# The block products of neighbouring column pairs in another order, raw weights in ten rotating homes, and a first pair computed K tile by K tile

## The chip, the core and the metric

The kernel runs on one core of a Trainium2 chip. Engines run beside each other: TensorE (PE, matmuls), VectorE (DVE) and ScalarE (ACT) for elementwise work, GpSimd (POOL) for some DMA issues, SyncE (SP) for most DMA issues. Each engine works through its own instructions in order, and semaphores tie the engines together. The metric is the device time of one execution in microseconds; the kernel before took 2662.76, 2666.23 and 2669.75 us in three runs (median 2666.23).

## What is computed

A trunk of two layers, each a half-step FFN, a token mixer (convolution, spatial gating, attention) and a second half-step FFN, for 576 tokens of width 1024. The change is in the FFNs; `D_FF` is 2816.

```python
def rms_norm(x, g):
    y = xf * lax.rsqrt(jnp.mean(xf * xf, axis=-1, keepdims=True) + EPS)
    return y.astype(x.dtype) * g
def swiglu(x, w_gu, w_down):
    gu = x @ w_gu
    return (jax.nn.silu(gu[..., :D_FF]) * gu[..., D_FF:]) @ w_down
def decoder_layer(...):
    x = x + 0.5 * swiglu(rms_norm(x, n1), gu1, dn1)
    m, ... = token_mixer(rms_norm(x, nm), ...)
    x = x + m
    x = x + 0.5 * swiglu(rms_norm(x, n2), gu2, dn2)
```

## The kernel before

Activations lie transposed, features on 128 partitions and the 576 tokens along the free axis, in two half columns of 288. A product in float32 quality takes three matmuls, since weights and activations are split into a high and a low part (`xh`, `xl`): high by high, high by low, low by high. K runs over 8 tiles of 128 for width 1024.

**Plain and block products.** The gate column and the up column of one index j (0 to 21) make a pair. Done plainly (`ftile`, lines 321 to 333, matmuls at L303, L306, L309), a pair takes 2 x 8 x 6 = 96 matmuls of 128x288. Only the first `N_PLAIN` = 2 pairs of the first FFN are done so. Every other pair is done as seven block products of 12 matmuls each (84), a scheme in the manner of Strassen: `product`, matmuls at L536, on sums of weight blocks and of activation blocks (`fac["b"]`, built by `post_x2`, `bottom`, `first_factors`). A pair needs a PSUM tile `z` with the two banks `z[:,0]` and `z[:,1]`, and a third bank `c`, called `n`. The seven products are called p1 to p7 here, by the bank that they add into:

- p1 into c (weights item q = 0), then ACT copies c into `z[:,0]`
- p5 into `z[:,1]` (q = 1), then ACT copies `z[:,1]` out into the buffer `p5`
- p6 into c (q = 3), then DVE writes `z[:,1]` = c + p5
- p2 into `z[:,0]` (q = 2)
- p7 into c (q = 4), then DVE writes u = c + p5
- p3 into `z[:,1]` (q = 5), then DVE writes g = z times the reciprocal norm `rstd`
- p4 into c (q = 6), then DVE takes u = c times `rstd` and finishes the pair (tanh on ACT, two products, a split into `ah` and `al`)

Each copy or sum between two products is a hand-over: the next product that writes one of its banks waits for it. `begin`, `middle` and `end` write the products of a pair; the scheduler orders instructions by priority, and the steady order on PE is p6(j), p1(j+1), p2(j), p5(j+1), p7(j), p3(j), p4(j).

**Weights.** A list `items` holds all weight pieces in order of use; `advance` loads each raw piece (256 KB) by a DMA on SP 4 items ahead of its preparation, and prepares it 7 items ahead of its use in the FFNs. To prepare is to split it: ACT writes the high part, DVE the low part (`by_vector`), or a DMA on POOL adds the raw piece onto minus the high part (`by_dma`, for q = 0, 2 and 6). The weights of the other four products are sums of raw blocks, made by DVE first (`sums`). Raw pieces live in `wr` (4 buffers), `cb` (4, shared with the mixer's convolution and its `ml`) and `vT` (1, shared with the attention); for pairs, the parity of j chooses `wr` or `cb`. The prepared forms rotate over the tags `w`, `sp`, `w`, `pt`.

**The FFN's start and end.** The 22 pairs are worked in four chunks; behind each chunk its products with the down projection (`w_dn`) follow. At the very start, x arrives tile by tile; ACT splits each tile and squares it (`post_x`), and the squares are summed on DVE. `rstd_steps` turns the sum into `rstd`: PE sums over partitions (`m<-ones,sq`), DVE does Newton steps on a 128x5 tile, PE spreads the result (`m<-idr,oh`), ACT copies it out. Behind the mixer the eight tiles of x come one by one out of the products with `w_out`, and `post_x2` builds the blocks from each.

Of the kernel before, what the change touches and what calls it, by code (L numbers as in the profile page):

```python
# [16 lines left out]
P = 128  # L17
# [23 lines left out]
W_G, W_C = (4, 4, 2, 3), (2, 3, 2)  # L41
CHUNKS = ((0, 6), (6, 12), (12, 17), (17, KF))

N_PLAIN = 2
# [51 lines left out]
def trunk(ctx: ExitStack, tc: tile.TileContext, a):  # L96
# [67 lines left out]
    def plain(ap, n, ff=False):  # L164
        for k0 in range(0, n, 4):
            items.append(("plain_ff" if ff else "plain", ap[:, k0:min(k0 + 4, n), :], min(n - k0, 4)))
# [4 lines left out]
    def ffn_items(l, f):  # L171
        j0 = N_PLAIN if l == 0 and f == 0 else 0
        for j in range(2 * j0):
            plain(a["w_gu"][l, f, j], 8, True)
        for k0, k1 in chunks(l, f):
            last = None
            for j in range(max(k0, j0), k1):
                for i, q in ((j, 0), (j, 1), (last, 4), (last, 5), (last, 6), (j, 3), (j, 2)):
                    if i is not None:
                        items.append(("pair", (l, f, i), q))  # L180
                last = j
            for q in (4, 5, 6):
                items.append(("pair", (l, f, last), q))
            for m in range(KD):
                plain(a["w_dn"][l, f, m, :, k0:k1, :], k1 - k0, True)

    for l in range(L):
# [12 lines left out]
        for i in range(8):  # L200
            plain(a["w_out"][l, i], 8)
        ffn_items(l, 1)
    state = {"load": 0, "prep": 0, "use": 0}
    state["form"] = 0
    raws, ready = {}, {}

    def load_raw(i):
        kind, what, n = items[i]

        def raw(key, ap, n, home="wr"):  # L210
            if home == "wr":
                t = wp.tile([P, 4, P], F32, tag="wr", name="wr", bufs=4)[:, 0:n, :]
            elif home == "cb":
                t = sp.tile([P, CB], F32, tag="cb", name="wc", bufs=4)[:, 0:n * P].rearrange("p (k m) -> p k m", k=n)
            else:
                t = sp.tile([P, 5, P], F32, tag="vT", name="wv")[:, 0:n, :]
# [5 lines left out]
        else:  # L222
            l, f, j = what
            for h, k in {0: ((0, 0),), 1: ((1, 0), (1, 4)), 2: ((0, 4),)}.get(n, ()):
                home = ("wr", "cb")[j % 2] if (h, k) != (1, 4) else ("wr", "cb", "vT")[j % 3]
                raw((what, h, k), a["w_gu"][l, f, 2 * j + h, :, k:k + 4, :], 4, home)

    def parts(ff, n):
        tag = "w"
        if ff:  # L230
            tag = ("w", "sp", "w", "pt")[state["form"] % 4]
            state["form"] += 1
# [20 lines left out]
    def prepare(i):  # L253
        kind, what, n = items[i]
        if kind != "pair":
            ready[i] = by_vector(raws.pop(i), n, kind == "plain_ff")
            return
        a11, a12, a21, a22 = (raws.get((what, h, k)) for h, k in ((0, 0), (0, 4), (1, 0), (1, 4)))
# [23 lines left out]
    def advance(i, look, raw=4):  # L282
# [38 lines left out]
    def ftile(rh, rl, z=None):  # L321
        z = z or ztile()
        zc = z if isinstance(z, list) else [z[:, c, 0:HT] for c in range(2)]
        k, nk = 0, len(rh)
        while k < nk:
# [4 lines left out]
            for g in list(chains):  # L330
                if next(g, "end") == "end":
                    chains.remove(g)
# [150 lines left out]
    for k in range(KD):  # L483
        sy.dma_start(out=x[k], in_=a["x"][:, k, :])
        if k in (0, 3):
            advance(0, 0 if k == 0 else 2, 0)
        post_x(k, 0, V_N1)
# [52 lines left out]
    def ffn(l, f, nxt):  # L540
        start = l == 0 and f == 0
        p5 = sp.tile([P, 2, 384], F32, tag="ws", name="p5")
        r = None
        for k0, k1 in chunks(l, f):
# [19 lines left out]
            def begin(what):  # L564

                b, j = fac["b"], what[2]
                z, c = ztile(), mtile("n")[:, h1]
                o = {"z": z, "c": c, "what": what, "p5": p5[:, j % 2, h1]}
                product(c, weights(what, 0), b[0], True)
                se.activation(out=z[:, 0, h1], in_=c, func=AF.Copy)  # L570
                product(z[:, 1, h1], weights(what, 1), b[1], True)
                se.activation(out=o["p5"], in_=z[:, 1, h1], func=AF.Copy)
                return o

            def middle(o):

                b, z, c, what = fac["b"], o["z"], o["c"], o["what"]
                product(c, weights(what, 3), b[3], False)
                ve.tensor_tensor(out=z[:, 1, h1], in0=c, in1=o["p5"], op=ALU.add)
                product(z[:, 0, h1], weights(what, 2), b[2], False)  # L580

            def end(o):

                b, z, c, what = fac["b"], o["z"], o["c"], o["what"]
                product(c, weights(what, 4), b[4], False)
                u = slot("t", "u")
                ve.tensor_tensor(out=u[:, h2], in0=c, in1=o["p5"], op=ALU.add)
                product(z[:, 1, h1], weights(what, 5), b[5], False)
                g, t = gate(z)
                product(c, weights(what, 6), b[6], False)  # L590
                silu(g, t)
                ve.tensor_tensor(out=u[:, h2], in0=u[:, h2], in1=r[:, h2], op=ALU.mult)
                ve.tensor_tensor(out=u[:, h1], in0=c, in1=r[:, h1], op=ALU.mult)
                keep(u, t)

            last = None
            for j in range(k0, k1):
                if start and j < N_PLAIN:
                    z = [ftile(xh, xl), ftile(xh, xl)]
                    if j == 0:  # L600
                        r = rms()
                        tops = first_factors()
                    g, t = gate(z[0])
                    silu(g, t)
                    u = slot("t", "u")
                    ve.tensor_tensor(out=half(u), in0=zf(z[1]), in1=half(r), op=ALU.mult)
                    keep(u, t)
                    if j == N_PLAIN - 1:
# [571 lines left out]
```

## Time and profile before

| what | value |
|---|---|
| three runs, median | 2666.23 us (2662.76 to 2669.75) |
| profiled execution: its own time, its span | 2666.37 us, 2664.6 us |
| busy: PE, DVE, ACT, POOL | 98%, 71%, 48%, 11% of the span |
| mean granted TensorE clock | 0.986 |
| chain of work that ended last | PE 82%, DVE 7%, DMA 7%, issue 3%, ACT 1% |

A matmul's row in the trace gives its start and its duration; matmuls overlap, so what one costs is read from starts or from a stretch with a count. The releaser in brackets behind a row is what ended the idle time ahead of it. A granted clock of 1.00 is 2.4 GHz, 0.50 is 1.2 GHz. PE is at 9 tenths or more in all of the page's 40 slices but the first.

### The profile page before, as it was taken

Reading aid. Unit: us, or ns where it says so; the run is one execution under the profiler, and the core shown is the slowest. Engines: PE = TensorE matmul, PEld = TensorE weight load, DVE = VectorE, ACT = ScalarE, POOL = GpSimd, SP = SyncE. Lnnn points to the kernel's source line nnn. Section 1 sums busy time; section 2 is a strip of 40 time slices with the busy share of each in tenths; the row PEclk is TensorE's granted clock in tenths of the full one; section 3 lists DMA queues with packets and bytes.
Section 4 is the critical chain, followed back from the end, with each engine's and each line's share of the span. In section 5 each row is a group of like instructions: output and inputs, shape, how many; then the busy total and the mean of one; then the engine's idle time right before and its main releaser. Section 6 shows DMA issues by size and latency. Waiting matters only on the chain.

```text
span 2664.6 us, 49246 instructions
## 1 busy us (share of the span) xinstructions
PE 2608.1 (98%) x18984; PEld 2533.2 (95%) x18984; DVE 1902.2 (71%) x3494; ACT 1283.6 (48%) x2423; POOL 291.6 (11%) x320
## 2 busy tenths in 40 slices
PE   6999999999999999999999999999999999999999
PEld 6999999988899989999989999999888999999999
DVE  6675665588898776756786766746888977756765
ACT  5454453335524464644674644533454245644543
POOL 0111110020010010111110111100200100111110
PEclk7999999989999999999999999999899999999999
DMA  5464554231222464654554645632312234645643
GB/s 166 113 152 120 131 123 135 81 92 57 60 82 82 122 143 120 151 124 119 134 129 117 151 119 124 135 126 84 82 56 68 84 91 128 151 119 133 138 122 100
DMA packets 194352, 304.08 MB, mean 114 GB/s; under 512 B 39482, under 2 KB 56762, under 8 KB 194116
## 3 DMA queue, kind: packets, MB, share of 16 engines
q1 hardware_dynamic: 156820, 233.28, 28.8%
q0 software_dynamic: 37152, 67.65, 15.2%
q8 instruction: 149, 2.44, 0.4%
q14 instruction: 87, 0.71, 0.1%
q10 hardware_dynamic: 144, 0.00, 0.0%
HBM read 221.43 MB, written 8.84 MB: 86 GB/s over the span
## 4 chain that ended last, share of the span: by engine, by line
PE 82%; DVE 7%; DMA 7%; issue 3%; ACT 1%; POOL 0%; SPq 0%; DVEq 0%; POOLq 0%; ACTq 0%
PE z L303 17%; PE z L306 17%; PE z L309 17%; PE n L536 13%; PE z L536 12%; PE n L86 4%; PE m L86 2%; DVE u L88 2%; DVE w L88 2%; DMA w<-wr 1%; DMA w<-wc 1%; DMA wv<-w_gu 1%; DMA w<-wv 1%; DMA wc<-w_gu 1%; DVE sums L88 1%
## 5 line engine op out<-in xcount | busy, mean ns | idle before, releaser
L88 ACT ACTIVATE w<-wr 128x512 fp32r<-128x512 f32 x762 | 433.5, 584 | 813.3 <-PE z L309 630.7
L536 PE MATMUL z<-xh,w 128*128 128x288 f32 x2064 | 455.8, 300 | 9.7 <-DVE z L88 6.5
L88 DVE TENSOR_TENSOR w<-wr,w 128x512 fp32r<-128x512 f32 (+2 forms) x528 | 321.3, 609 | 160.4 <-ACT w L88 159.5
L536 PEld LDWEIGHTS z<-xh,w 128*128 128x128 f32 x2064 | 343.6, 189 | 24.6 <-DVE z L88 13.4
L303 PE MATMUL z<-xh,w 128*128 128x288 f32 x1504 | 336.3, 305 | 13.5 <-ACT w L88 9.7
L88 DVE TENSOR_TENSOR w<-sums,w 128x512 fp32r<-128x512 f32 x344 | 235.4, 688 | 148.4 <-ACT w L88 145.9
L309 PE MATMUL z<-xh,w 128*128 128x288 f32 x1504 | 326.8, 298 | 0.1
L306 PE MATMUL z<-xl,w 128*128 128x288 f32 x1504 | 326.7, 299 | 0.0
L536 PE MATMUL z<-xl,w 128*128 128x288 f32 x1032 | 305.2, 296 | 0.0
L536 PE MATMUL n<-fh,w 128*128 128x288 f32 x1376 | 304.7, 295 | 0.1
L303 PE MATMUL z<-ah,w 128*128 128x288 f32 x1408 | 303.0, 297 | 0.0
L306 PE MATMUL z<-al,w 128*128 128x288 f32 x1408 | 301.8, 296 | 0.0
L309 PE MATMUL z<-ah,w 128*128 128x288 f32 x1408 | 301.1, 296 | 0.0
L303 PEld LDWEIGHTS z<-xh,w 128*128 128x128 f32 x1504 | 245.6, 193 | 26.8 <-issue 10.1
L88 ACT ACTIVATE w<-sums 128x512 fp32r<-128x512 f32 x344 | 212.9, 623 | 121.0 <-PE z L309 76.0
L306 PEld LDWEIGHTS z<-xl,w 128*128 128x128 f32 x1504 | 247.1, 192 | 0.9 <-issue 0.7
L309 PEld LDWEIGHTS z<-xh,w 128*128 128x128 f32 x1504 | 246.2, 192 | 0.8 <-issue 0.3
L88 DVE SCALAR_TENSOR_TENSOR c<-cb,vec,c 128x512 f32<-128x512 f32 x480 | 243.5, 553 | 0.1
L536 PEld LDWEIGHTS n<-fh,w 128*128 128x128 f32 x1376 | 230.8, 188 | 0.6 <-DVE w L88 0.3
L303 PEld LDWEIGHTS z<-ah,w 128*128 128x128 f32 x1408 | 226.4, 189 | 3.2 <-ACT ah L88 3.2
L309 PEld LDWEIGHTS z<-ah,w 128*128 128x128 f32 x1408 | 226.5, 189 | 0.0
L306 PEld LDWEIGHTS z<-al,w 128*128 128x128 f32 x1408 | 226.4, 189 | 0.0
(244 smaller groups left out, 4598.2 us busy)
## 6 DMA issues: line engine op xcount, KB each, us to landing
wr<-w_in SPq DMA_DIRECT2D x184, 256.0 KB, 2.8
wr<-w_gu SPq DMA_DIRECT2D x168, 256.0 KB, 3.0
wc<-w_gu SPq DMA_DIRECT2D x156, 256.0 KB, 3.0
wr<-w_dn SPq DMA_DIRECT2D x128, 256.0 KB, 2.7
w<-wr POOLq DMA_DIRECT2D x117, 256.0 KB, 3.9
w<-wc POOLq DMA_DIRECT2D x113, 256.0 KB, 3.9
wr<-w_dn SPq DMA_DIRECT2D x64, 128.0 KB, 2.4
wr<-w_out SPq DMA_DIRECT2D x32, 256.0 KB, 2.8
```

Of the source, the lines that this page charges most:

```text
L86: r = f(*args, **kw)
L88: r = f(*args, **kw)
L303: pe.matmul(out=z[c], lhsT=wh, rhs=rh[:, s], start=first, stop=False)
L306: pe.matmul(out=z[c], lhsT=wh, rhs=rl[:, s], start=False, stop=False)
L309: e = pe.matmul(out=z[c], lhsT=wl, rhs=rh[:, s], start=False, stop=last)
L536: e = pe.matmul(out=out, lhsT=w[:, k, :], rhs=r, start=first and k == 0 and i == 0, stop=k == n - 1 and i == 2, skip_group_check=True)
```

## The change

In the steady loop the products of two neighbouring pairs are issued in a new order: p6(j), p5(j+1), p2(j), p7(j), p1(j+1), p3(j), p4(j); c alternates between the PSUM tags `n` and `m` (two buffers each); the scheduler puts the last matmul of p5(j+1) behind p2(j). The `p5` buffer moves from the tag `ws` to a slot of `e`. Raw pieces of the FFNs rotate over ten homes (four `wr`, `vT`, `ws`, four `cb`), and loads run 6 items ahead in place of 4. Three pairs are plain; of the first pair both products are computed together, K tile by K tile, the squares of x come behind all splits, and the first product of the second pair goes into two `n` banks while `rstd` is made. Of the first two down products of a chunk, the first four K tiles come ahead of and behind the last p4. The weights `w_out` are looked ahead and stored as the FFNs' are; the third wait count `W_G` of the spatial gating is 3 in place of 2. PE runs 18716 matmuls in place of 18704.

```diff
-W_G, W_C = (4, 4, 2, 3), (2, 3, 2)
+W_G, W_C = (4, 4, 3, 3), (2, 3, 2)
-N_PLAIN = 2
+N_PLAIN = 3
...
     def ffn_items(l, f):
...
+            if j == 0:
+                for n in (4, 8):
+                    for h in range(2):
+                        plain(gu[h], n, "plain_ff", n - 4)
...
             for j in range(max(k0, j0), k1):
-                for i, q in ((j, 0), (j, 1), (last, 4), (last, 5), (last, 6), (j, 3), (j, 2)):
+                for i, q in ((j, 0), (j, 1)) if last is None else ((j, 1), (last, 4), (j, 0), (last, 5), (last, 6)):
+                    items.append(("pair", (l, f, i), q))
+                for q in (3, 2):
+                    items.append(("pair", (l, f, j), q))
...
-            plain(a["w_out"][l, i], 8)
+            plain(a["w_out"][l, i], 8, "plain_out")
...
+            if kind in ("pair", "plain_ff"):
+                home = ("wr", "vT", "wr", "ws", "wr", "cb", "wr", "cb", "cb", "cb")[state["raw"] % 10]
+                state["raw"] += 1
...
-                home = ("wr", "cb")[j % 2] if (h, k) != (1, 4) else ("wr", "cb", "vT")[j % 3]
-                raw((what, h, k), a["w_gu"][l, f, 2 * j + h, :, k:k + 4, :], 4, home)
+                raw((what, h, k), a["w_gu"][l, f, 2 * j + h, :, k:k + 4, :], 4)
...
-            tag = ("w", "sp", "w", "pt")[state["form"] % 4]
+            tag = ("sp", "w", "pt", "w")[state["form"] % 4]
...
-            ready[i] = by_vector(raws.pop(i), n, kind == "plain_ff")
+            ready[i] = by_vector(raws.pop(i), n, kind != "plain")
...
-    def advance(i, look, raw=4):
+    def advance(i, look, raw=6):
...
-            advance(0, 0 if k == 0 else 2, 0)
-        post_x(k, 0, V_N1)
+            advance(0, 1 if k == 0 else 3, 0)
+        split(x[k], xh[k], xl[k], vcol(0, V_N1 + k))
+    for k in range(KD):
+        square(k)
...
-        p5 = sp.tile([P, 2, 384], F32, tag="ws", name="p5")
+        p5s = slot("e", "p5").rearrange("p (i n) -> p i n", i=2)
...
+            def plainly(j):
+                if j == 0:
+                    z = [ztile(), ztile()]
+                    for n in (0, 4):
+                        hl = [weights(), weights()]
+                        for k in range(4):
+                            for (h, lo, _), y in zip(hl, z):
+                                mark["mm"] = mm3([y[:, c, 0:HT] for c in range(2)], h[:, k, :], lo[:, k, :],
+                                                 xh[n + k], xl[n + k], n + k == 0, n + k == 7)
...
+                    g = rstd_steps(acc["t"], 1.0 / D, EPS, r, w=1)
+                    chains.append(g)
+                    first.append(ftile(xh, xl, [mtile("n")[:, h1] for c in range(2)]))
+                    drain(g)
...
+                if j == 1:
+                    tops = first_factors()
+                if j == N_PLAIN - 1:
+                    first_tops(tops)
...
-                o = begin((l, f, j))
-                if last:
-                    end(last)
-                middle(o)
+                o = {"what": (l, f, j), "z": ztile(), "c": mtile("n" if j % 2 else "m")[:, h1], "p5": p5s[:, j % 2, h1]}
+                if last is None:
+                    p1(o)
+                    p5(o)
+                    seed(o)
+                    save(o)
+                else:
+                    p5(o)
+                    save(o)
+                    p7(last)
+                    p1(o)
+                    seed(o)
+                    p3(last)
+                    p4(last)
+                p6(o)
+                p2(o)
...
-            end(last)
+            p7(last)
+            p3(last)
+            for m in range(2):
+                g = ftile_parts(ah, al, None, k1 - k0)
+                dn.append((next(g), g))
+                next(g)
+                if m == 0:
+                    p4(last)
```

`seed` is the ACT copy of c into `z[:,0]`, `save` the ACT copy of `z[:,1]` into the `p5` buffer; `ftile_parts` is `ftile` as a generator that stops behind each piece of four K tiles.

Three places as the programs have them. The first is PE at the very start; `z_181` and `z_186` are the first gate product, `z_269` and `z_187` the up product of the same pair, `xh0` to `xh3` the tiles of x. Before:

```order
L303 MATMUL z_181<-xh0_72,w_107 128x288 x2
L306 MATMUL z_181<-xl0_80,w_107 128x288 x2
L309 MATMUL z_181<-xh0_72,w_107 128x288 x2
L303 MATMUL z_181<-xh1_73,w_107 128x288 x2
L306 MATMUL z_181<-xl1_81,w_107 128x288 x2
L309 MATMUL z_181<-xh1_73,w_107 128x288 x2
L303 MATMUL z_181<-xh2_74,w_107 128x288 x2
```

After:

```order
L322 MATMUL z_186<-xh0_72,w_107 128x288 x2
L325 MATMUL z_186<-xl0_80,w_107 128x288 x2
L328 MATMUL z_186<-xh0_72,w_107 128x288 x2
L322 MATMUL z_187<-xh0_72,w_112 128x288 x2
L325 MATMUL z_187<-xl0_80,w_112 128x288 x2
L328 MATMUL z_187<-xh0_72,w_112 128x288 x2
L322 MATMUL z_186<-xh1_73,w_107 128x288 x2
```

Each tile of x now feeds 12 matmuls where it fed 6 before the next tile is needed.

The second is PE in one steady pair of the last FFN, the first row of each product. Before, p6, p1 of the next pair, p2, p5 of the next, p7, p3, p4:

```order
L536 MATMUL n_28777<-fh_24930,w_28742 128x288
...
L536 MATMUL n_28916<-xh0_72,w_28778 128x288
...
L536 MATMUL z_28776<-xh4_76,w_28759 128x288
...
L536 MATMUL z_28915<-xh0_72,w_28796 128x288
...
L536 MATMUL n_28777<-fh_24930,w_28814 128x288
...
L536 MATMUL z_28776<-xh4_76,w_28833 128x288
...
L536 MATMUL n_28777<-f4_24648,w_28856 128x288 x6
```

After, p6, p5 of the next pair, p2, the last matmul of that p5, p7, p1 of the next, p3, p4:

```order
L569 MATMUL m_28770<-fh_24948,w_28735 128x288
...
L569 MATMUL z_28908<-xh0_72,w_28774 128x288
...
L569 MATMUL z_28769<-xh4_76,w_28752 128x288
...
L569 MATMUL z_28908<-xh3_75,w_28774 128x288
L569 MATMUL m_28770<-fh_24948,w_28794 128x288
...
L569 MATMUL n_28909<-xh0_72,w_28811 128x288
...
L569 MATMUL z_28769<-xh4_76,w_28830 128x288
...
L569 MATMUL m_28770<-f4_24665,w_28849 128x288 x6
```

p1 of the next pair went from between p6 and p2 to between p7 and p3; p5 of the next pair took its place. The same pair on DVE, from u = c + p5 to the sum into `z[:,1]` of the next pair. Before:

```order
L88 TENSOR_TENSOR u_28968<-n_28777,p5_25175 128x288
L88 TENSOR_TENSOR sums_24651<-wr_28852,wr_28831 128x512
L88 TENSOR_TENSOR w_28972<-sums_24651,w_28972 128x512
L88 TENSOR_TENSOR g_28987<-z_28776,rstd_25270 128x576
L88 TENSOR_TENSOR u_28968<-u_28968,rstd_25270 128x288
L88 TENSOR_TENSOR sums_24651<-wr_28951,sums_24651 128x512
L88 TENSOR_TENSOR u_28968<-n_28777,rstd_25270 128x288
...
L88 TENSOR_TENSOR z_28915<-n_28916,p5_25175 128x288
```

After:

```order
L88 TENSOR_TENSOR u_28948<-m_28770,p5_25190 128x288
L88 TENSOR_TENSOR sums_24668<-wr_28790,wr_28828 128x512
L88 TENSOR_TENSOR u_28948<-u_28948,rstd_25263 128x288
L88 TENSOR_TENSOR w_28969<-sums_24668,w_28969 128x512
L88 TENSOR_TENSOR g_28984<-z_28769,rstd_25263 128x576
L88 TENSOR_TENSOR sums_24668<-wc_28910,sums_24668 128x512
L88 TENSOR_TENSOR u_28948<-m_28770,rstd_25263 128x288
...
L88 TENSOR_TENSOR z_28908<-n_28909,p5_25190 128x288
```

The product of u with `rstd` moved ahead of g; in the rows left out both have t, w and u.

The third is SP where the last FFN's loads begin, with what each load waits for. Before:

```order
L88 DMA wr_24893<-w_gu 128x512 [waits DMAHW7_49,DVE_49]
L88 DMA wr_24941<-w_gu 128x512 [waits DMAHW0_49,DVE_49]
...
L88 DMA wr_25196<-w_gu 128x512 [waits DMAHW4_49,DVE_49]
L88 DMA wc_25047<-w_gu 128x512 [waits PE_49]
L88 DMA wc_25096<-w_gu 128x512 [waits PE_49]
```

After:

```order
L88 DMA wr_24706<-w_gu 128x512 [waits DMAHW4_49,DMAHW0_49,DVE_49]
L88 DMA wr_24842<-w_gu 128x512 [waits DMAHW1_49,DVE_49]
...
L88 DMA wr_25113<-w_gu 128x512 [waits DMAHW7_49,DMAHW3_49,DVE_49]
L88 DMA wc_24745<-w_gu 128x512 [waits PE_49]
L88 DMA wc_24747<-w_gu 128x512 [waits PE_49]
```

Loads into `wc` (the `cb` buffers) wait for PE in both, since the mixer's `ml` lies there until its last products; the pieces that wait (`wc_24745`, `wc_24747`) are now two of the first pair's own blocks.

## Rows read from the trace of the kernel before

**Rows 1.** Windows by stage: stretch, us, PE busy (matmuls), granted clock, DMA share, GB/s.
```profile
0.00:63.58 63.58, 42.97 (x237) 0.79 0.56 170
63.58:434.19 370.61, 367.21 (x2715) 1.00 0.54 131
434.19:940.23 506.04, 501.98 (x3635) 0.98 0.29 85
940.23:1346.99 406.76, 398.76 (x2926) 0.99 0.55 131
1346.99:1751.09 404.10, 397.54 (x2926) 1.00 0.55 133
...
2257.02:2664.60 407.58, 397.50 (x2926) 1.00 0.53 127
```
**Rows 2.** Windows of a stretch without waits and of two at half clock.
```profile
733.87:810.02 76.15, 76.15 (x579) 1.00 0.26 83
944.80:951.70 6.90, 5.40 (x22) 0.51 0.30 63
30.00:54.00 24.00, 14.98 (x56) 0.50 0.31 85
```
**Rows 3.** Waits of PE over the whole run: us in total, times, longest.
```profile
PE n L536 <- DMA w<-wc: 11.2, 4, 4.1
PE z L303 <- ACT w L88: 9.7, 2, 6.5
PE z L536 <- DVE z L88: 6.5, 18, 0.4
PE n L536 <- DVE u L88: 5.3, 6, 2.2
PE m L86 <- ACT oh L337: 5.2, 2, 3.3
PE z L303 <- DVE g L88: 3.8, 1, 3.8
PE n L536 <- DMA w<-wr: 3.1, 1, 3.1
```
**Rows 4.** Timeline of the start, PE and ACT: start us, us, engine, line, tile.
```profile
6.51 0.85 PE L303 MATMUL z<-xh,w 128*128 128x288 f32 x2 [6.51 <-ACT w L88]
...
12.37 2.10 ACT L88 ACTIVATE xh<-x,vec 128x576 fp32r<-128x576 f32 x3
...
38.87 0.85 PE L536 MATMUL n<-xh,w 128*128 128x288 f32 x2 [3.22 <-DMA w<-wc]
...
48.19 0.85 PE L303 MATMUL z<-xh,w 128*128 128x288 f32 x2 [3.77 <-DVE g L88]
```
**Rows 5.** Timeline of the norm in the first mixer, PE.
```profile
446.88 1.17 PE L86 MATMUL m<-ones,sq 128*128 128x1 f32 x10
...
451.24 1.53 PE L86 MATMUL m<-idr,oh 128*128 128x128 f32 x10
```
**Rows 6.** Timeline of a steady pair with a wait, then of one without.
```profile
1086.45 0.37 PE L536 MATMUL n<-xh,w 128*128 128x288 f32 x1
...
1088.67 0.40 PE L536 MATMUL z<-xh,w 128*128 128x288 f32 x1 [0.41 <-DVE z L88]
...
1107.72 0.45 DVE L88 TENSOR_TENSOR u<-u,rstd 128x288 f32<-128x288 f32 x1
...
1110.99 0.46 DVE L88 TENSOR_TENSOR z<-n,p 128x288 f32<-128x288 f32 x1
...
1111.61 0.29 PE L536 MATMUL z<-xh,w 128*128 128x288 f32 x1
```
**Rows 7.** Timeline of the p4 that waited longest.
```profile
1392.18 3.25 PE L536 MATMUL n<-f,w 128*128 128x288 f32 x12 [2.25 <-DVE u L88]
```
**Rows 8.** Timeline of an FFN's start behind the mixer, DVE.
```profile
943.73 0.69 DVE L88 TENSOR_TENSOR sums<-wc 128x512 f32<-128x512 f32 x1 [1.23 <-DMA wc<-w_gu]
...
948.71 0.75 DVE L88 TENSOR_TENSOR fl<-u,fh 128x576 fp32r<-128x576 f32 x1
```

## What the change should do to the time

> **What bounds the kernel now.** I read the page first: PE is busy 98% of the span and makes 82% of the chain that ended last. Time can go only where PE stands, where its clock is low, or where matmuls are saved. None is saved here: the change adds 12. So I read the windows by stage [rows 1] against a stretch in which PE never waits [rows 2]: 579 matmuls in 76.15 us, 0.132 us each. A stage's loss is its length minus its count of matmuls times 0.132. The start loses 63.58 - 237 x 0.132 = 32.3 us, the first FFN 370.61 - 2715 x 0.132 = 12.2, the three later FFNs 406.76, 404.10 and 407.58 less 2926 x 0.132 = 386.2 each, so 20.5, 17.9 and 21.4; the mixer shown loses 26.2. That is what a change of order can work on: 32 us in one place and 72 over four FFNs.
>
> Next the waits of PE [rows 3] say what those losses are. Waits on DVE's z are p2's, behind the sum c + p5: 18 times, 6.5 us. Waits on DVE's u are p4's: 6 times, 5.3. The waits on w<-wc (11.2), w<-wr (3.1), ACT's w (9.7) and DVE's g (3.8) lie in the start and at the beginnings of the FFNs. A wait costs more than its own length: between the first matmuls of p1 and p2 lie 2.22 us in the pair with a wait [rows 6] where 12 x 0.132 = 1.58 would do, so 0.64 for a wait shown as 0.41. And where PE stood longest the granted clock fell to 0.50 or 0.51, the lower of its two levels: 22 matmuls in 5.40 us, 0.245 each [rows 2].
>
> **The start.** PE begins at 6.51 [rows 4] whatever comes later. ACT splits a tile of x in 0.70 us (2.10 for three [rows 4]). In the old order a tile feeds 6 matmuls of the first product, 0.79 us; now 12, 1.58, and the squares no longer stand on ACT between the splits, so from the second tile on PE should not wait for x. The third plain pair and the delayed factors put the first block product later, which gives its weights time: the waits 3.1 on w<-wr and 3.2 on w<-wc should go, as should the second wait on ACT's w (9.7 - 6.5 = 3.2). The wait of 3.8 on g [rows 3, 4] goes because the third product has banks of its own. What stays, or comes, I estimate as: 6.5 before the first matmul; 2 for the first tiles at half clock (some 18 matmuls at 0.245 - 0.132); 1.4 until the sum of squares, now behind all splits, is there (0 to 3); 2.0 for the chain of the norm. That chain takes 4.36 from its first to its second matmuls in the mixer [rows 5]; at the start four more large DVE operations of about 0.45 [rows 6] can stand inside, so 6.2, against a cover of 24 matmuls (3.2) and the ten small ones (1.17 [rows 5]). Then 1.2 until g frees the next product's banks, and 2 for a spell of low clock behind these waits (0 to 6). Sum 15.1 in place of 32.3; less 12 x 0.132 = 1.6 for the added matmuls, the start gains 15.5. Without any wait for squares or low clock it is 19, rounded up to 20; with the upper ends (3, 6), a norm wait of 4 and half of the two waits for weights returning (3) it is 5.
>
> The low clock is the term I trust least. The 24.0 us at 0.50 [rows 2] cost, by the rows, 56 x (0.245 - 0.132) = 6.3 of slower matmuls; the rest is waiting. The Trainium skill (TensorE: Matmul & The Clock Gate, section Terms) puts the penalty at the throttled time times (1 - K/N), here 12.0, as if PE were busy throughout. If the new start kept such a spell and filled it, as that page supposes, the 2 above would be 12 and the sum 2641. The trace disagrees with 12.0 for the old start, since PE issued only 56 matmuls in it.
>
> **p2 behind the sum into z.** In the steady pair one product stands between p6 and p2 in both orders, so the margin hardly changes by the order alone. Without a wait the sum ends at 1110.99 + 0.46 = 1111.45 and p2 starts at 1111.61 [rows 6]: 0.16 us of slack. On DVE everything from g to the sum is one unbroken run; the product of u and rstd (0.45 long, about 0.37 of issue) moves from inside that run to ahead of g, while p5 of the next pair leaves its last matmul behind p2 (0.13 less). New slack: 0.16 + 0.37 - 0.13 = 0.40. The waits of before come where a sum of raw blocks waits for its load and pushes g late; loads are now issued 6 items ahead into ten homes, so most should be early. 18 x 0.64 = 11.5 lost now; I take 9 of it as gained (bounds 3 to 12).
>
> **p4 behind u.** p7 writes c, DVE reads it, p4 writes it again. Before, only p3 (1.58 us) lay between; now p1 and p3 lie there, 3.17. The six waits average 0.9, the longest 2.25 [rows 3, 7], so 1.58 more cover takes all but the longest. They cost 5.3, about 0.28 each around it as at p2 (1.7), and 3.25 - 1.58 = 1.7 of low clock behind the longest [rows 7]: 8.7. Gain 7 (4 to 8).
>
> **The FFNs' beginnings.** Waits on w<-wc were 11.2 in four places, 3.2 of it in the start [rows 3, 4], so 8.0 at the three later FFNs; with low clock behind them (22 x 0.113 = 2.5 [rows 2], in two of three) 13 to 16. Earlier loads shorten the first; but the first pair's blocks now include pieces in `cb` buffers, which SP may fill only when the mixer's last products have left them. I take a gain of 5, with -5 and 11 as ends.
>
> **New short hand-overs.** p7 follows p6 by 24 matmuls where it was 36, and the copy out of p5 by ACT has less to hide behind. Nothing of this waits by the durations above, as 3.17 us covers a 0.46 us sum many times. I charge 1; the upper end is 85 block pairs at 0.1 = 8.5.
>
> **Edits at nothing.** The third count of the spatial gating moves transposes of one group, while the wait on ACT's oh (5.2 [rows 3]) stands behind the same matmul as before; the forms and look-ahead of w_out and the p5 buffer's new place lie beside PE work in a mixer that is 0.98 of full clock [rows 1]. Ends -4 and 4. The early down products stand behind the last p4 of a chunk with the same count of matmuls, and give that p4 more cover (counted above).
>
> **Sum.** 15.5 + 9 + 7 + 5 - 1 = 35.5. From the profiled execution's 2666.37 (span 2664.6 and 1.8 around it; the median of the runs is 2666.23, so no correction), 2631.
>
> **Rivals.**
> R1, the steady waits stay. The order gives p2 no more cover, and if DVE runs late for its own load and not for the raw pieces, p2 and p4 wait as before; only the start gains: 2666.4 - 15.5 = 2651. For it: DVE works without a gap from g to the sum [rows 6]. Against it: p4's cover doubles by the order itself.
>
> R2, the FFNs' beginnings get worse. DVE stands at 943.73 for 1.23 us behind a load, with x's own evacuation and fl (ends 949.46) queued behind such sums [rows 8]. If the new homes make a sum wait for a `cb` load that itself waits for the mixer's last products, the last blocks of x come later by about 3.3 us, at three FFNs 10 in place of the gain of 5: 2631 + 15 = 2646. The Trainium skill (TensorE: Matmul & The Clock Gate, section Architectural detail) calls ACT's and DVE's queues strictly first in, first out; the trace agrees, nothing passed the sum at 943.73. By that rule R2 holds wherever such a sum stands ahead of x.
>
> R3, slower: DVE is late in every pair. The slack is a few tenths of a microsecond. If the run from g to the sum takes over 0.40 longer (one more large operation that slips in, for which 0.45 [rows 6] is the size), p2 waits in each pair that has one ahead of it in its chunk, 85 less 16 chunk beginnings, 69. At 0.64 plus a little, 0.67, that is 46 in place of 11.5: instead of gaining 9, p2 loses 34.5, and p4, which hangs on the same engine, gains none of its 7. 2631 + 43.5 + 7 = 2681. It decides from 0.40 us on: below that no p2 waits, above it all do.
>
> R1 with R2: 2651 + 10 = 2661, no change that shows.
>
> **How the numbers follow.** Forecast 0.62, R1 0.14, R2 0.08, R3 0.10, R1 with R2 0.06. The likeliest case's own range, from the ends of its terms: all best 2666.4 - (20 + 12 + 8 + 11 + 4) = 2611, rounded to 2612; several terms at their low ends together, 2645. The range of 8 in 10 reaches from there over R1 and R2 to 2658 and leaves out R3, R1 with R2 and a little of the tail. Within 0.3% (8 us, about what a measurement of this kernel can tell from none) lie 2658 to 2674: that is R1 with R2, 0.06. Faster 0.84, slower 0.10.
>
> **What would show it.** The window of the start: the first steady block product comes with some 17 us less loss, no wait on w<-wr or w<-wc in it, no second wait on ACT's w. In the waits of PE: DVE z under 2 us in total, DVE u under 1. On the timeline of a steady pair, p2 starting with no bracket behind p5. Behind the mixers, a wait on w<-wc below 2 us. R1 shows as 18 or more waits on DVE z with the start short; R2 as a longer idle time of PE on fl or w at 941 to 951's counterparts, and low clock there; R3 as some 69 waits on DVE z. The prediction is wrong if the start still loses over 27 us, if the waits on DVE z grow, or if a hand-over that is not in the old list (p1's copy, p5's save) appears with over 8 us.

## The result and the profile after

The changed kernel takes 2622.78 us (median of 4 runs, 2618.08 to 2624.13), the kernel before 2664.49 over the runs made with it: ratio 0.9839, 95% interval 0.9817 to 0.9862. The profiled execution has a span of 2621.9 us where it had 2664.6, so 42.7 us are to be found in the traces. The forecast was 2631 with a range of 2612 to 2658: the way was right, and the kernel came out 8 us faster than forecast (35.5 us of gain forecast, 42.7 found).

The windows of the changed kernel by the same stages (stretch, us, PE busy (matmuls), granted clock, DMA share, GB/s); the first ends where the first steady block product begins, now behind three plain pairs:

```profile
0.00:53.13 53.13, 44.30 (x308) 0.97 0.61 192
53.13:416.73 363.60, 358.48 (x2654) 1.00 0.56 134
416.73:920.61 503.88, 500.40 (x3635) 0.99 0.29 86
920.61:1315.96 395.35, 392.96 (x2927) 1.00 0.56 134
1315.96:1711.89 395.93, 393.12 (x2926) 1.00 0.56 135
...
2216.29:2621.90 405.61, 394.41 (x2926) 1.00 0.53 128
```

Beside [rows 1]: start and first FFN together went from 434.19 to 416.73 us with 12 more matmuls, the second FFN from 406.76 to 395.35, the third from 404.10 to 395.93, the fourth only from 407.58 to 405.61, the first mixer from 506.04 to 503.88. Count times 0.132 leaves 9, 10 and 19 us lost in the last three FFNs. The fourth is the odd one, and the waits of PE in the changed kernel begin to say why:

```profile
PE z L322 <- ACT w L88: 6.6, 1, 6.6
...
PE z L569 <- DVE z L88: 3.7, 8, 0.6
PE n L569 <- DVE u L88: 2.0, 2, 1.7
PE z L569 <- DVE x L88: 1.8, 2, 1.2
PE n L569 <- ACT w L88: 1.5, 1, 1.5
PE n L569 <- DMA w<-wr: 1.5, 1, 1.5
...
PE m L569 <- DMA w<-wc: 1.0, 1, 1.0
...
PE m L569 <- DVE u L88: 0.6, 2, 0.3
```

Against [rows 3], p2's waits (DVE z) fell from 18 to 8, p4's (DVE u, on `n` and on `m`, since c alternates) from 6 to 4 and from 5.3 to 2.6 us, the 11.2 us on w<-wc to 1.0, and the second wait on ACT's w in the start is gone. Of the rows left, ACT's w on n, w<-wr and one of the two on DVE x lie in the first 15 us of the fourth FFN.

For a finer account I gave every matmul of both traces its product by the program's order, took the time from one start to the next less 0.132 us, and summed it by product. Behind the first 60 matmuls of each FFN (its beginning, counted apart), in us, four FFNs together:

| loss ahead of or in | before | changed | gained | forecast |
|---|---|---|---|---|
| start; changed: with the first 60 block matmuls, and 1.6 for 12 more matmuls | 32.3 | 15.9 + 1.6 | 14.8 | 15.5 |
| beginnings of the three later FFNs | 16.4 | 10.7 | 5.7 | 5 |
| p2 | 17.6 | 10.9 | 6.7 | 9 |
| p4 | 11.1 | 5.5 | 5.6 | 7 |
| p1 and p5 | 11.6 | 1.6 | 10.0 | -1, with p6 |
| p6 | 2.5 | 5.6 | -3.1 | in the row above |
| two mixers | 52.4 | 48.7 | 3.7 | 0 |

These make 43.4 of the 42.7; the down products and the norms lost a little. A sum of this kind hangs by some 0.7 us on how a matmul at the border of two products is counted. DVE shows the same from the other side. Its waits for raw loads ahead of the block sums, before:

```profile
DVE sums L88 <- DMA wr<-w_gu: 44.5, 19, 3.6
DVE sums L88 <- DMA wv<-w_gu: 29.2, 11, 4.1
...
DVE sums L88 <- DMA wc<-w_gu: 21.4, 10, 4.6
```

and in the changed kernel, where wc is the name of the pieces in cb, in vT and in ws:

```profile
DVE sums L88 <- DMA wc<-w_gu: 20.9, 23, 3.7
...
DVE sums L88 <- DMA wr<-w_gu: 2.6, 4, 0.7
```

The link between these waits and PE's can be read in the rows. Here is a late load before, with the p4 and the p2 that follow it:

```profile
367.45 0.69 DVE L88 TENSOR_TENSOR sums<-wc,wr 128x512 f32<-128x512 f32 x1 [2.58 <-DMA wr<-w_gu]
...
369.17 1.86 PE L536 MATMUL n<-f,w 128*128 128x288 f32 x12 [0.18 <-DVE u L88]
...
374.68 0.40 PE L536 MATMUL z<-xh,w 128*128 128x288 f32 x1 [0.41 <-DVE z L88]
```

and one in the changed kernel:

```profile
229.18 0.69 DVE L88 TENSOR_TENSOR sums<-wc 128x512 f32<-128x512 f32 x1 [2.14 <-DMA wc<-w_gu]
...
230.90 1.85 PE L569 MATMUL n<-f,w 128*128 128x288 f32 x12 [0.23 <-DVE u L88]
...
236.41 0.40 PE L569 MATMUL z<-xh,w 128*128 128x288 f32 x1 [0.60 <-DVE z L88]
```

I counted this over whole traces. DVE stands over 1 us for a raw load 37 times before (92.7 us) and 8 times in the changed kernel (14.9). Take the steady p4 that begin over 0.15 us after their turn: all 9 before and all 4 in the changed kernel come within 3.2 us behind the end of such a wait. Of the steady p2 that begin over 0.2 us late, 20 of 21 before and 5 of 6 in the changed kernel have one in the 8 us ahead of them; of the p2 in time, 3 of 44 and 1 of 64. So both waits follow late loads, before and after.

### The profile page after: what moved, and what is told of

It is laid out like the page before. It is cut to its first block, busy times and chain, and to the rows that moved or that the text cites. A ratio compares the mean times of both kernels' runs of the same rounds, so it can differ in the third digit from the quotient of the medians.

```text
span 2621.9 us, 49387 instructions
## 1 busy us (share of the span) xinstructions
PE 2584.4 (99%) x18996; PEld 2519.7 (96%) x18996; DVE 1909.9 (73%) x3488; ACT 1273.5 (49%) x2415; POOL 286.9 (11%) x317
## 4 chain that ended last, share of the span: by engine, by line
PE 91%; DVE 3%; DMA 3%; issue 1%; ACT 1%; SPq 0%; POOL 0%; DVEq 0%; POOLq 0%; ACTq 0%
PE z L322 18%; PE z L325 17%; PE z L328 17%; PE z L569 14%; PE n L569 9%; PE m L569 9%; PE n L86 4%; PE m L86 2%; DMA wc<-w_gu 2%; DMA w<-wc 1%; DVE w L88 1%; ACT w L88 1%; DVE u L88 0%; DVE sums L88 0%; DVE x L88 0%
## 5 line engine op out<-in xcount | busy, mean ns | idle before, releaser
L88 ACT ACTIVATE w<-wr 128x512 fp32r<-128x512 f32 (+1 forms) x533 | 324.0, 622 | 657.9 <-PE z L328 526.2
L88 ACT ACTIVATE w<-wc 128x512 fp32r<-128x512 f32 (+2 forms) x509 | 271.5, 565 | 243.3 <-PE z L328 89.1
L88 DVE TENSOR_TENSOR w<-wr,w 128x512 fp32r<-128x512 f32 (+2 forms) x373 | 254.3, 682 | 122.0 <-ACT w L88 121.5
L88 POOL DMA_DIRECT2D w<-wc x175 | 150.5, 860 | 616.6 <-ACT w L88 221.3
```

Source lines behind the costliest of these rows:

```text
L88: r = f(*args, **kw)
```

## The experiments

The theory: three parts of the change work, each in its place: the ten homes (raw loads land earlier), the order of the block products (more cover for p4 and for the copies), and the new start. Each was taken out alone, then the homes were put alone into the old kernel, then the beginnings of the FFNs were tried. The order alone and the start alone were not put into the old kernel. The kernel before, measured again beside each of three groups of kernels, had medians of 2663.1, 2663.6 and 2663.9 us, so the medians below can be compared across groups.

**Old order.**
```diff
-                for i, q in ((j, 0), (j, 1)) if last is None else ((j, 1), (last, 4), (j, 0), (last, 5), (last, 6)):
...
+                for i, q in (j, 0), (j, 1), (last, 4), (last, 5), (last, 6):
...
+                p1(o)
+                seed(o)
+                p5(o)
+                save(o)
+                if last is not None:
                     p7(last)
-                    p1(o)
-                    seed(o)
                     p3(last)
                     p4(last)
```
The list of weight pieces, and with it the order of the raw loads, goes back too.

> The changed kernel with the steady order of the block products of the kernel before (p6, p1 of the next pair, p2, p5 of the next, p7, p3, p4); all else as changed, c alternating between two tags included. Theory A (the order itself gives p1, p5 and p4 their cover): the losses ahead of p1 and p5 in the steady pairs, 11.6 us before and 1.6 in the changed kernel, and ahead of p4 (11.1 and 5.5) come back: 12 to 16 us over the changed kernel, some 2635 to 2639. Rival B (the earlier loads and the ten homes carry the steady gain, the order little): under 4 us, 2623 to 2627, and p2's waits do not grow under either.

Measured 2635.73 us, ratio to before 0.9900 (0.9876 to 0.9923): 13 over the changed kernel, as theory A has it, but not for all of its reasons. Its waits:

```profile
PE z L570 <- DVE z L88: 6.6, 16, 0.5
...
PE z L570 <- ACT z L88: 6.0, 5, 2.3
```

those of its weight loads (PEld) and those of DVE:

```profile
PEld z L570 <- ACT z L88: 12.8, 32, 2.5
...
DVE sums L88 <- DMA wr<-w_gu: 37.7, 19, 3.9
...
DVE sums L88 <- DMA wc<-w_gu: 11.0, 17, 2.1
```

16 waits of p2 are back (18.5 us lost by product where 10.9 were), against what both theories said. The rows of DVE say why: the loads are late again. DVE's sums wait 48.7 us for them where the changed kernel has 23.5, 16 times for over 1 us where it has 8, and 14 of the 17 late p2 have such a wait in the 8 us ahead of them, of the 48 in time only one. So the order counts for p2 through the loads; why it makes them earlier is not shown. p5's loss is back too (7.6). Its weight loads wait for ACT's copy into z, 26 times behind the beginnings of the FFNs, 23 of them in the first pairs of a chunk, about 0.2 us each; the five waits in PE's own row on ACT z all lie in the first 60 block matmuls of an FFN. p4 loses 6.9, only 1.4 more, and p1 nothing. The beginnings of the three later FFNs lose 17.9 us where the changed kernel's lose 10.7, which neither theory had. This trace is of the slowest of the four runs (2643.39 us), so its losses are some 8 us more than the median's.

**Old homes, loads 4 items ahead.**
```diff
-                home = ("wr", "vT", "wr", "ws", "wr", "cb", "wr", "cb", "cb", "cb")[state["raw"] % 10]
...
+                home = ("wr", "cb")[j % 2] if (h, k) != (1, 4) else ("wr", "cb", "vT")[j % 3]
...
-    def advance(i, look, raw=6):
+    def advance(i, look, raw=4):
```


> The changed kernel with the raw homes of the kernel before (parity of j chooses wr or cb, vT every third, down weights in wr) and loads 4 items ahead. Theory A (waits of p2 and the stalls at the FFNs' beginnings come from late raw loads): p2's loss rises from 11 to about 17, the three later beginnings from 10.7 to about 16: 8 to 13 us over the changed kernel, 2631 to 2636. Rival B (with the new order a late load is hidden): within 3 us of it, 2620 to 2626.

Measured 2641.99, ratio 0.9927 (0.9907 to 0.9946): 19 over the changed kernel, more than theory A's 8 to 13. Rival B is out. The waits of PE

```profile
PE z L566 <- DVE z L88: 11.6, 22, 0.9
...
PE m L566 <- DVE u L88: 5.5, 9, 1.5
```

and of DVE

```profile
DVE sums L88 <- DMA wr<-w_gu: 49.7, 26, 3.4
DVE sums L88 <- DMA wc<-w_gu: 34.7, 25, 3.2
```

show it: the sums wait 84 us for raw loads where the changed kernel has 23.5, and p2 and p4 wait behind them (25.0 and 12.2 us by product, worse than in the kernel before). The new order does not cover them: DVE stands 38 times for over 1 us, and 24 of the 25 late p2 and all 16 late p4 follow such a wait. The start loses 5.3 more up to its 600th matmul. The three later beginnings, though, lose 6.9 us and not the 16 that theory A expected, and the fourth FFN's fell from 5.2 to 0.8: in the old homes the first pair's four pieces all lie in wr.

**Look-ahead alone.** Ten homes, `raw=4`.

> The changed kernel with raw loads 4 items ahead as before, in the ten homes. Theory A (the homes bring the gain that the old homes lost, 19 us): within 4 us of the changed kernel, 2621 to 2627. Rival B (the look-ahead brings it, homes only make room for it): 12 to 19 us more, with p2's and p4's waits as in the kernel with old homes.

Measured 2619.10, ratio 0.9830 (0.9813 to 0.9846): theory A. With loads 4 ahead in both, ten homes against the old ones are worth 23 us (2641.99 to 2619.10); the longer look-ahead brings nothing that shows.

**Old start.** `N_PLAIN = 2`, one product after the other, `post_x` with its squares between the splits, `rms()` behind the first pair.

> The changed kernel with the old start: two plain pairs, one product after the other, squares between the splits, the norm after the first pair. Theory A (the start is worth what the windows show, 32.3 against 12.5 us lost, less 1.6 for 12 more matmuls and 3 of waits moved behind it): 13 to 18 us over the changed kernel, 2636 to 2641, with idle rows of 3 us on w<-wr, w<-wc and g back. Rival B (most of it came from the ten homes and earlier loads, which this kernel keeps): 3 to 8 us, 2626 to 2631.

Measured 2628.00, ratio 0.9872 (0.9857 to 0.9887): 5 over the changed kernel, rival B's range. PE's timeline shows a long wait on the norm, where the kernel before waited for weights and for g [rows 4]:

```profile
22.13 1.17 PE L86 MATMUL m<-ones,sq 128*128 128x1 f32 x10
...
31.67 2.56 PE L86 MATMUL m<-idr,oh 128*128 128x128 f32 x10 [8.36 <-ACT oh L88]
```

Up to the 600th matmul this kernel loses 28.0 us, the changed one 17.1, the one before 33.5. So of the start's 14.8, the start's own edits give 28.0 - 17.1 - 1.6 = 9.3 and the homes 5.3; the medians differ by less (5), as later stages vary (this run's fourth FFN was 2.2 us shorter than the changed kernel's, its first mixer 3.8 longer) and the trace is of the slowest of the four runs (2631.64). The wait on g came back (2.9 us), but none on w<-wr or w<-wc, which theory A had asked for.

**Mixer edits.** `W_G` third count 2, w_out as the mixer's other weights.

> The changed kernel with the third count of W_G back to 2 and the w_out items looked ahead and stored as the mixer's other weights. Theory A (these two edits made the mixers 2.2 and 1.5 us shorter): both mixers longer by that, 2625 to 2628. Rival B (the mixers are shorter through what the FFNs leave behind, or by chance): within 1.5 us of the changed kernel, mixers unchanged.

Measured 2623.80, ratio 0.9853 (0.9839 to 0.9868): rival B. The two edits are worth nothing that shows. Over the traces of the changed kernel and its variants the first mixer lasts between 500.6 and 507.7 us and the second between 501.9 and 506.5, and before's (506.0 and 505.9) lie inside: the 3.7 us of the table are no finding.

**Homes alone, in the kernel before** (with its p5 buffer in the tag `e`).

> The kernel before with the ten rotating raw homes alone (the p5 buffer moved to the tag e to make room), loads 4 items ahead, old order, old start. Theory A (the waits of p2 need both cures, the new order's 0.24 us of slack and early loads; with the old order and the ten homes they were 19.3 us lost): the start gains about 5 and p4 about 4, p2 and p5 nothing: 2651 to 2658. Rival B (the homes carry by themselves the 19 us that taking them out cost): 2643 to 2648.

Measured 2651.33, ratio 0.9954 (0.9941 to 0.9966): theory A. Its waits:

```profile
PE n L540 <- DMA w<-wr: 11.8, 3, 4.1
...
PE n L540 <- DMA w<-wc: 6.1, 1, 6.1
PE z L540 <- DVE z L88: 5.9, 14, 0.6
```

Taking the homes out costs 19 us, putting them in alone gives 13: 14 of p2's waits stay without the new order. DVE stands 17 times for over 1 us for a raw load (42.7 us), as with the old order and the new start (16, 39.4). So the long waits for loads are 37 or 38 with the old homes in either order, 16 or 17 with the ten homes and the old order, and 8 with both. The rows on w<-wr and w<-wc lie in the start (6.1 and 3.5 us) and at the two beginnings behind a mixer (4.1 each).

**One tag for c.** `mtile("n")` for every pair.

> The changed kernel with c always in the tag n (two buffers) in place of n and m by turns. Theory A (the order gives p1 its room: its bank's last reader, u, lies 24 matmuls and more back): p1 loses as little as in the changed kernel, 0.5 us, time within 3 us of it. Rival B (the four buffers do it): p1's waits of the kernel before come back, 3 to 4 us more.

Measured 2621.86, ratio 0.9845 (0.9831 to 0.9858): theory A; four buffers for c are not needed.

**More work on DVE between g and the sum.** `u = c * r` taken twice, then three times.

> The changed kernel with u = c times rstd taken twice in each block pair, the same operation and the same result: one more VectorE operation of 0.45 us (about 0.37 of issue) between g and the sum into z. The scheduler answers by putting p5's last and two matmuls of the next p1 ahead of p2, 0.40 us more cover. Theory A (p2 waits only where the run from g to the sum passes the slack of about 0.40): slack 0.40 + 0.40 - 0.37 = 0.43, no new waits, within 3 us of the changed kernel. Rival B (VectorE's load as such sets the time): 85 x 0.37 = 31 us more.

> The changed kernel with u = c times rstd taken three times in each block pair (two more operations, 0.74 us of issue between g and the sum); in this program p2 follows p6 and twelve matmuls of p5, 0.13 us more cover than in the changed kernel. Theory A: slack 0.40 + 0.13 - 0.74 = -0.21, so p2 waits in about 69 pairs, 0.21 plus some 0.28 around each wait: 34 us more, 2653 to 2662. Rival B (the waits come from late raw loads alone and the run's length does not count): within 4 us of the changed kernel.

Measured 2626.72, ratio 0.9853 (0.9832 to 0.9875), and 2635.69, ratio 0.9892 (0.9870 to 0.9914). With two, theory A's 3 us were 4, and rival B is out. With three, p2 did not wait (7 waits on DVE z), because the scheduler put the sum ahead of u times t:

```profile
1078.25 0.46 DVE L88 TENSOR_TENSOR z<-n,p 128x288 f32<-128x288 f32 x1
1078.61 0.75 DVE L88 TENSOR_TENSOR u<-u,t 128x576 f32<-128x576 f32 x1
```

The run from the start of g to the start of the sum was 3.94 us where the changed kernel has 3.88, 0.06 us longer and not 0.74 as I had reckoned. So this run doesn't test the slack. The 13 us went elsewhere, to down products that wait for DVE to take x out of their banks:

```profile
PE z L322 <- DVE x L88: 7.9, 17, 0.7
```

**The FFNs' beginnings.** The rotation begun anew at each FFN, then only at the two behind a mixer (with `raw=4`).
```diff
+            if n == 0 and j == 0 and f == 1:
+                state["raw"] = 0
...
-    def advance(i, look, raw=6):
+    def advance(i, look, raw=4):
```
(The first of the two kernels has the condition without `f == 1`, and `raw=6`.)

> The changed kernel with the rotation of the ten raw homes begun anew at each FFN, so that the first pair's four raw pieces lie in wr, vT, wr and ws and none waits for a cb buffer that the mixer's last products still hold. Theory A (the stalls at the FFNs' beginnings come from those cb loads and the sums queued behind them on VectorE ahead of x): the loss over the first 60 matmuls of the three later FFNs, 2.2, 3.4 and 5.2 us in the changed kernel, falls to about 1 to 1.5 each: 5 to 7 us less, 2616 to 2618. Rival B (the beginnings are late through the eight tiles of x themselves): within 2 us of the changed kernel.

> The changed kernel with the rotation of the raw homes begun anew only at the two FFNs behind a mixer, and loads 4 items ahead. Begun anew at every FFN, the two beginnings behind a mixer fell from 2.2 and 5.2 us lost to about 0.5 each, but the one behind an FFN rose from 3.4 to 5.3. Theory A (only cb buffers held by a mixer's last products matter; behind an FFN the rotation had better run on): 2 us under the kernel with every FFN begun anew, 2608 to 2612. Rival B (the third FFN's beginning differs by chance): as that kernel, 2612 to 2615, its beginning at 5.

Measured 2612.57, ratio 0.9809 (0.9792 to 0.9827), and 2607.80, ratio 0.9798 (0.9783 to 0.9813). Both are faster than theory A's ranges (2616 to 2618, 2608 to 2612). The second is the fastest kernel here, 15 us under the changed one by the medians and 11 under the changed one with loads 4 ahead (2619.10). In the changed kernel the fourth FFN begins so (the first PE row of its products is at 2216.29):

```profile
2210.64 5.10 SPq L88 DMA_DIRECT2D wc<-w_gu  x5
...
2217.04 0.69 DVE L88 TENSOR_TENSOR w<-sums,w 128x512 fp32r<-128x512 f32 x1 [0.39 <-ACT w L88]
...
2221.11 0.40 PE L569 MATMUL n<-xh,w 128*128 128x288 f32 x1 [1.48 <-ACT w L88]
...
2221.40 0.75 DVE L88 SCALAR_TENSOR_TENSOR x<-z,x 128x576 f32<-128x576 f32 x1
```

Five loads into wc come in one burst 6 us ahead of use, when the mixer's last products let the cb buffers go. Each FFN takes 152 raw pieces by the program's lists, so here the rotation stands at its seventh home, and three of the first pair's four pieces fall into cb (at the second FFN one, at the third two). The sums that need them stand on DVE ahead of the last tile of x, which is taken out 5.1 us after PE has begun the block products. With the rotation begun anew (PE starts at 2207.85):

```profile
2209.30 0.75 DVE L88 SCALAR_TENSOR_TENSOR x<-z,x 128x576 f32<-128x576 f32 x1
```

it is taken out after 1.45 us. The first pair's pieces now lie in wr, vT, wr and ws. The beginnings lose 0.6 (second FFN), 3.3 (third) and 0.5 (fourth) where they lost 2.2, 3.4 and 5.2. Begun anew at the third too, that one lost 5.3; in the eight traces with the new order and the ten homes in which the rotation runs on into it, it loses 3.3 to 3.6, so rival B's chance is out and theory A holds there as well. The medians of the two kernels differ by more than these 2 us (4.8), but their look-ahead differs too. p2's and p4's losses in the fourth FFN fell with it (1.8 and 0.4, from 4.1 and 1.5). Of the 18.1 us between the two traces 6.4 lie in the beginnings and 5 in the fourth FFN behind its beginning; 4.5 lie in the mixers, within what these vary by.

## Why the prediction came out as it did

**The start** (15.5 forecast, 14.8 found) was right in its sum and in most of its terms:

```profile
24.41 1.28 PE L86 MATMUL m<-ones,sq 128*128 128x1 f32 x10
...
29.39 1.70 PE L86 MATMUL m<-idr,oh 128*128 128x128 f32 x10 [0.82 <-ACT oh L88]
...
32.46 0.53 PE L322 MATMUL z<-xh,w 128*128 128x288 f32 x2 [1.37 <-DVE g L88]
```

First matmul 6.6 (forecast 6.5), the first twelve matmuls 2.99 us, 1.4 over 12 x 0.132 (2), the norm's wait 0.82 (2.0), the release by g 1.37 (1.2), no wait for the squares (1.4); the norm's chain took 29.39 - 24.41 = 4.98 us, not 6.2. Not in the sum were 3.3 us in the first block products, where a wait on w<-wc came back at a third of its length (1.0 for 3.2). The cause was half wrong: the step credits the third plain pair and the products taken K tile by K tile with all of it, and the runs give them 9.3 and the homes 5.3. The spell of low clock (2) came, and short, behind the two waits:

```profile
33.00:53.00 20.00, 20.00 (x141) 0.91 0.19 43
```

That is 20.00 - 141 x 0.132 = 1.4 us, where the old start had 0.50 over 24 us [rows 2]. The Trainium skill's rule (TensorE: Matmul & The Clock Gate, section Terms) would give, as an estimate, 0.09 / 0.5 x 20 = 3.6 us at half speed, times one half, 1.8: with PE busy throughout, as here, rule and rows nearly agree, where for the old start they differed by half.

**p2** (9, found 6.7): right in its cause, the late loads, and too large in size, since 8 waits stayed (3.7 us, where the prediction's sign asked for under 2), again behind late loads. Wrong was what it said of the order. It saw there a change of slack, 0.16 to 0.40, and gave the earlier loads to look-ahead and homes alone; the look-ahead brought nothing, and with the ten homes the order halves the number of long waits for loads (16 to 8). The slack itself is not 0.40 either. In an undisturbed pair of the changed kernel:

```profile
1069.06 0.46 DVE L88 TENSOR_TENSOR u<-m,rstd 128x288 f32<-128x288 f32 x1 [0.22 <-PE m L569]
...
1071.37 0.46 DVE L88 TENSOR_TENSOR z<-n,p 128x288 f32<-128x288 f32 x1
...
1071.93 0.36 PE L569 MATMUL z<-xh,w 128*128 128x288 f32 x1
```

p2 starts 0.10 us behind the sum's end (1071.83), as it does in 44 of the 54 steady pairs counted. That is not more than before, where it was 0.10 to 0.17 in most pairs without a wait (0.16 in the one that the prediction took). What the order gave is that DVE stands 0.22 us for the end of p4, so that g may be late by that much more: 0.32, counted as the prediction counted. That this margin is worth anything by itself no run shows.

**p4** (7, found 5.6): near in size, wrong in its cause. The step gave the order the credit, by 1.58 us more cover. With the order taken back p4 loses only 1.4 us more, with the homes taken back 6.7 more. Against a late load the new order covers p4 less: u stands on DVE behind the sum that waits, and where DVE waited 2.58 us for a load, p4 waited 0.18 before, and where it waited 2.14 us, p4 waited 0.23 in the changed kernel (the rows above). The gain is that fewer loads are late. What is left is one wait of 1.7 us and one small one in the first FFN and two small ones in the fourth.

**The short hand-overs** (-1, found 6.9): the step that failed, the term of the sum that was mis-sized. I looked for what p6, p7 and the copies would newly lose, and found 3.1 at p6; I left out what p1 and p5 would gain. In the old order p5 follows ACT's copy of p1's bank into the other half of its tile; PE's own row for it (z behind ACT z, 2.9 us, 5 times) lies but for one wait in the beginnings, which are counted apart. The row that shows it is that of the weight loads, which I passed over; before, and then in the changed kernel:

```profile
PEld z L536 <- ACT z L88: 9.2, 31, 1.8
```

```profile
PEld m L569 <- ACT z L88: 2.6, 7, 1.5
PEld n L569 <- ACT z L88: 2.5, 8, 1.1
```

Before, 26 of the 31 stand ahead of p5 behind the beginnings, 5.2 us in all, 23 of them in the first pairs of a chunk. In the changed kernel none stands ahead of p5 and 14 of the 15 ahead of p6, 12 of these in the first pairs of a chunk: the wait for the copy moved in part from p5 to p6, which is where p6's 3.1 come from in the main. The old order brought 6.4 of p5's 6.8 back. p1's 3.2 came back neither with the old order nor with one tag for c, so either cure is enough for it (homes alone, with neither, left p1 losing 3.4).

**The FFNs' beginnings** (5, found 5.7): right in sum. Rival R2 was there all the same, in one FFN of three: the fourth, at 2221.40, is its mechanism in the main, sums on cb loads ahead of x, though DVE works through them in one run there and does not stand for a load. It is the 5 us that the last experiment takes out. The trace agrees there too with the rule of the Trainium skill that the prediction quotes (TensorE: Matmul & The Clock Gate, section Architectural detail), that DVE's queue is strictly first in, first out: at 2217.04 DVE had stood 0.39 us for ACT's part of a weight, and x, whose last products start at 2216.03 and end at 2216.45, did not pass.

**Edits at nothing**: right for `W_G` and w_out, by the run without them. The other edits at nothing (the p5 buffer's place, the rotation of the forms, the early down products) were not taken out alone.

**R1** fell: the steady waits did not stay. With the new order and the old homes they do (22 of p2, 11 of p4). **R3** did not come: 8 waits, not 69. Its threshold of 0.40 us could not be tried in a clean form, since the scheduler reorders both DVE and PE around an added operation.

Taken out one at a time, order, homes and start cost 13, 19 and 5 us, 37 of the 42 by medians; the forecast's parts, 15.5, 9, 7, 5 and -1, came near in sum through errors of both signs, and that is luck in part: the hand-overs' 7.9 us too little stand against 2.3, 1.4 and 0.7 too much at p2, p4 and the start.

## What to carry to other kernels

A wait that several things feed (here p2 and p4: late loads, whose number hangs on the homes and on the order together) is not priced by one of them; take out each part alone and put one in alone before a gain is given a name. And follow a wait back on the engine that releases it: PE's rows name DVE's sum, DVE's rows some 7 us earlier name the load. When buffers are shared between stages, look at which of the next stage's first loads fall into buffers that the last stage frees last, and begin the rotation there anew: two lines of code for it, with loads again 4 ahead, took the kernel from 2622.8 us (2619.1 with loads 4 ahead alone) to 2607.8. When a term is "short hand-overs", list the old waits of the same kind first, those of the weight loads too: what they give back counts as much as what the new ones cost.

## What was not expected of the hardware

The granted clock can fall even behind short waits: behind the 8.36 us wait of the old start it was 0.60 over 23 to 40 us, behind waits of 0.82 and 1.37 us in the changed kernel 1.00 from 29 to 33 us and 0.91 from 33 to 53, and behind a single wait of 1.7 us, at p4 in the first FFN, 0.66 from 339 to 344 us. But it need not: behind waits of 1.2 us (926 to 937, 1319 to 1335) and around two of 1.5 (2220 to 2236) it stayed at 1.00.

```profile
339.00:344.00 5.00, 4.42 (x22) 0.66 0.83 195
...
2220.00:2236.00 16.00, 12.24 (x87) 1.00 0.60 138
```

What decides between the two is not shown here.
